# A softmax load of which one row is sent over 126 and 2 partitions, so that DMA engines 14 and 15 carry less

## Chip, cores and metric

One core of one Trainium2 chip. Times are device microseconds of one launch. Executions are sorted into a fast and a slow state by their time and clock. A comparison runs a kernel and the kernel before in turn on the same chip; its ratio has a 95% interval. The kernel before had 162.26 us (162.17 to 162.34, 3 runs) when the prediction was made.

## The reference

```python
def reference(x):                     # x: 16 x 1024 x 512, float32
    x_scaled = x / 2.0
    x_max = np.max(x_scaled, axis=-1, keepdims=True)
    exp_x = np.exp(x_scaled - x_max)
    return (exp_x / np.sum(exp_x, axis=-1, keepdims=True)).astype(np.float32)
```

33.55 MB are read and as many written.

## The kernel before

The 16384 rows are cut into 12 tiles of 3, 7, 15 ... 15, 7, 3 and 3 rows per partition. A tile is loaded by one DMA over 128 partitions, worked on in place and stored by one DMA. Eight loads are issued from the scalar engine at the start; stores and the last four loads come from the sync engine, so there are two queues. The vector engine takes the maximum (`do_max`), the scalar engine the exponential and its sum, the vector engine multiplies by the reciprocal.

```python
PLAN = [
    ([3], 0), ([4, 3], 3), ([5] * 3, 10), ([5] * 3, 25), ([5] * 3, 40), ([5] * 3, 55),
    ([5] * 3, 70), ([5] * 3, 85), ([5] * 3, 10), ([4, 3], 3), ([3], 0), ([3], 25),
]
# ... cut
    def issue_loads(begin, end):
        for t in range(begin, end):
            if t not in behind:      # behind: tiles whose place another tile must leave first
                nc.scalar.dma_start(out=sb(t), in_=dram(xf, t)).then_inc(ld[t], 16)

    def do_max(k):
        t, b, c, a = chunks[k]
        nc.vector.reduce_max(
            out=negmax[:, b : b + c], in_=arena[:, a : a + c],
            axis=mybir.AxisListType.X, negate=True,
        )._wait_ge(ld[t], 16).then_inc(s_max, 1)
# ... cut: reciprocal, multiply, exponentials
        for t in range(len(tiles)):
            nc.sync.wait_ge(s_mul, last_chunk[t] + 1)
            nc.sync.dma_start(out=dram(of, t), in_=sb(t)).then_inc(
                st[t] if t in awaited else s_end, 16
            )
            # ... cut: late loads, each behind the stores that free its place
```

## Time and profile before

| | before |
|---|---|
| time, us | 162.26 |
| span of the profiled execution, us | 161.7 (that execution took 163.47 in all) |
| vector / scalar engine busy, us | 131.7 / 94.5 |
| end of the vector engine's work, us | 143.6 |
| end of the last DMA data packet, us | 160.29 |

How the profile is read stands in the prediction. The profiled execution was 1.2 us longer than the timed ones.

### The profile page before, as it was taken

The numbers are of one execution on the slowest core, as the hardware profiler recorded it, in microseconds if no ns is written. First come the engines' busy times: TensorE is split into PE (matmuls) and PEld (weight loads), VectorE is DVE, ScalarE is ACT, GpSimd is POOL, SyncE is SP. The second block draws the span as 40 slices with busy tenths as digits, with TensorE's granted clock in tenths as the row PEclk, the third lists the DMA queues.
The fourth block names the chain that finished last, engine by engine and source line by source line (L and its number), as shares of the span: only waits on it lengthen the run. The fifth ranks groups of instructions, "written<-read, shape, count | busy, mean of one in ns | idle before, by whom it ended". The sixth has DMA issues, their size and how long they took to land.

```text
span 161.7 us, 480 instructions
## 1 busy us (share of the span) xinstructions
DVE 131.7 (81%) x155; ACT 94.5 (58%) x257; POOL 0.2 (0%) x4
## 2 busy tenths in 40 slices
DVE  0475599999999999999999999999999999950000
ACT  0739086748646745976667866668766875600000
POOL 0000000000000000000000000000000000000000
DMA  7989999899999899999999999999999899999991
GB/s 283 464 388 464 410 436 438 326 466 404 473 380 479 372 486 410 441 448 405 456 395 471 388 471 405 448 399 457 409 412 482 388 471 426 426 448 403 414 414 53
DMA packets 3459, 67.13 MB, mean 415 GB/s; under 512 B 384, under 2 KB 384, under 8 KB 1152
## 3 DMA queue, kind: packets, MB, share of 16 engines
q1 hardware_dynamic: 2304, 40.90, 59.0%
q10 hardware_dynamic: 1152, 26.21, 38.5%
q14 instruction: 3, 0.02, 0.0%
HBM read 33.55 MB, written 33.55 MB: 415 GB/s over the span
## 4 chain that ended last, share of the span: by engine, by line
DVE 77%; DMA 10%; issue 0%; DVEq 0%
DVE negmax L89 40%; DVE arena L109 22%; DVE arena L102 13%; DMA arena<-in_x_dram 10%; DVE recip L98 2%; DVEq L204 0%
## 5 line engine op out<-in xcount | busy, mean ns | idle before, releaser
L122 ACT ACTIVATE arena<-arena,negmax 128x512 f32<-128x512 f32 x128 | 90.7, 710 | 42.6 <-DVE negmax L89 42.6
L89 DVE TENSOR_REDUCE negmax<-arena 128x5 f32<-128x2560 f32 (+2 forms) x28 | 72.3, 2585 | 10.9 <-DMA arena<-in_x_dram 10.9
L109 DVE TENSOR_SCALAR arena<-arena,recip 128x512 f32<-128x512 f32 x91 | 37.8, 482 | 0.7
L122 ACT ACTIVATION_READ_ACCUMULATOR arena<-arena,negmax 128x1 f32 x128 | 23.9, 187 | 0.0
L102 DVE TENSOR_TENSOR arena<-arena,recip 128x2560 f32<-128x2560 f32 (+2 forms) x8 | 21.0, 2625 | 0.3
L98 DVE RECIPROCAL recip<-sums 128x5 f32<-128x5 f32 (+2 forms) x28 | 4.9, 176 | 0.0
L122 ACT ACT_TABLE_LOAD x1 | 1.3, 1283 | 4.6 <-issue 4.6
L193 POOL MEMSET const-bfloat16-1.0<- 128x1 bf16 x1 | 0.1, 102 | 0.0
L193 POOL MEMSET const-uint8-127<- 128x1 uint8 x1 | 0.1, 102 | 0.0
L193 POOL MEMSET const-float32-0.0<- 128x1 f32 x1 | 0.1, 99 | 0.2 <-issue 0.2
L193 POOL MEMSET const-float32-1.0<- 128x1 f32 x1 | 0.1, 99 | 0.0
## 6 DMA issues: line engine op xcount, KB each, us to landing
out_dram<-arena SPq DMA_DIRECT2D x7, 3840.0 KB, 22.9
arena<-in_x_dram ACTq DMA_DIRECT2D x6, 3840.0 KB, 46.9
arena<-in_x_dram SPq DMA_DIRECT2D x1, 3840.0 KB, 30.4
out_dram<-arena SPq DMA_DIRECT2D x2, 1792.0 KB, 16.6
out_dram<-arena SPq DMA_DIRECT2D x3, 768.0 KB, 15.8
arena<-in_x_dram ACTq DMA_DIRECT2D x1, 1792.0 KB, 8.3
arena<-in_x_dram SPq DMA_DIRECT2D x1, 1792.0 KB, 34.0
arena<-in_x_dram SPq DMA_DIRECT2D x2, 768.0 KB, 34.8
```

Of the source, the lines that this page charges most:

```text
L89: nc.vector.reduce_max(out=negmax[:, b : b + c], in_=arena[:, a : a + c], axis=mybir.AxisListType.X, negate=True,)._wait_ge(ld[t], 16).the ...
L98: nc.vector.reciprocal(out=recip[:, b : b + c], in_=sums[:, b : b + c])._wait_ge(s_exp, k + 1).then_inc(s_rec, 1)
L102: nc.vector.tensor_mul(out=arena[:, a : a + c], in0=arena[:, a : a + c], in1=recip[:, b : b + c].unsqueeze(2).to_broadcast([P, c, D]),)._w ...
L109: ins = nc.vector.tensor_scalar_mul(out=arena[:, a + r], in0=arena[:, a + r], scalar1=recip[:, b + r : b + r + 1],)
L122: ins = nc.scalar.activation(out=arena[:, a + r], in_=arena[:, a + r], func=mybir.ActivationFunctionType.Exp, bias=negmax[:, b + r : b + r ...
L193: nc = _bacc.Bacc("TRN2", target_bir_lowering=False, num_devices=1)
```

## The change

The intent is to take work off DMA engines 14 and 15. One row of the second load goes over 126 partitions by a DMA of its own, and the last two partitions of that row by a third DMA; the prediction says why this should spare engines 14 and 15.

```diff
+SPREAD = 1
@@ issue_loads
-            if t not in behind:
+            if t == SPREAD:
+                r = tiles[t][1] - 1
+                for p, q, lo, hi in ((0, P, 0, r), (0, 126, r, r + 1), (126, P, r, r + 1)):
+                    nc.scalar.dma_start(
+                        out=sb(t)[p:q, lo:hi], in_=dram(xf, t)[p:q, lo:hi]
+                    ).then_inc(ld[t], 16)
+            elif t not in behind:
                 nc.scalar.dma_start(out=sb(t), in_=dram(xf, t)).then_inc(ld[t], 16)
@@ do_max
-        )._wait_ge(ld[t], 16).then_inc(s_max, 1)
+        )._wait_ge(ld[t], 48 if t == SPREAD else 16).then_inc(s_max, 1)
```

## The prediction

> **What bounds the kernel now.** I read the first two parts of the page first: the busy shares and the forty slices of about 4.04 us each.
>
> ```profile
> span 161.7 us, 480 instructions
> DVE 131.7 (81%) x155; ACT 94.5 (58%) x257; POOL 0.2 (0%) x4
> DVE  0475599999999999999999999999999999950000
> ACT  0739086748646745976667866668766875600000
> DMA  7989999899999899999999999999999899999991
> HBM read 33.55 MB, written 33.55 MB: 415 GB/s over the span
> ```
>
> The reader is to see that the vector engine falls silent four slices (some 17 us) before the end, while the DMA row stays at 9 until the last slice. Transfers end this kernel, not arithmetic. The chain of waits on the page says "DVE 77%" and hides this: its last piece is a vector multiply that ends near 143.6 us, because the final wait for all stores is not followed back to a transfer. So I left the chain and looked at the window sums (columns: stretch, its length, busy time of the three engines, clock, DMA share, GB/s).
>
> ```profile
> 1.00:1.50 0.50, 0.00 (x0) 0.00 (x0) 0.00 (x0) 1.00 1.00 172
> 1.50:2.00 0.50, 0.00 (x0) 0.00 (x0) 0.00 (x0) 1.00 0.56 184
> ...
> 157.00:157.60 0.60, 0.00 (x0) 0.00 (x0) 0.00 (x0) 1.00 1.03 430
> 157.60:158.20 0.60, 0.00 (x0) 0.00 (x0) 0.00 (x0) 1.00 0.50 205
> 158.20:158.80 0.60, 0.00 (x0) 0.00 (x0) 0.00 (x0) 1.00 0.27 113
> 158.80:159.40 0.60, 0.00 (x0) 0.00 (x0) 0.00 (x0) 1.00 0.12 51
> 159.40:160.30 0.90, 0.00 (x0) 0.00 (x0) 0.00 (x0) 1.00 0.05 20
> ```
>
> The tail is the point. Up to 157.6 us all 16 DMA engines work; then the share falls to 0.50, 0.27, 0.12 and 0.05, and 0.05 of 16 engines is less than one engine. The end of the kernel is set by one DMA engine that is late, over two microseconds after most of the others. The change shifts bytes between engines, so only this imbalance can pay.
>
> **Which engine is late.** The trace also holds every packet (start, duration, size) and every semaphore increment of a DMA, but not the engine's number. I joined packets into 16 series, each packet following the end of another by at most a few ns. The first packets of the first load start at 1.14 to 1.47 us on fourteen engines and at 2.00 and 2.02 us on two. The increments of the second load arrive at a median of 8.21 us; the last three are 0.37, 0.62 and 0.68 us behind it. So two engines are some 0.65 us late there, and keep it: the third load has two at 0.86 and 0.88, the fourth two at 1.07. In the last phase, when one queue alone is left, the last increments lie 0.57, 0.81, 0.87 and 1.48 us behind the median at 106 us, and 0.62, 0.86, 1.34 and 2.22 us at the very end (median 158.4 us). The step from 1.48 to about 2.2 and from 0.87 to about 1.35 comes near 111 to 112 us, where a few 6144-byte load packets take 402 to 915 ns in place of 234. The 16 series end at 160.29, 159.40, 158.94, 158.69, and the rest from 157.6 to 158.2 us.
>
> **What the Trainium skill says.** In "DMA: Bandwidth & Descriptors", section "Why a DMA increments its semaphore by 16 and not by 1", a DMA issued from the scalar or sync engine runs on the largest k up to 16 that divides the slowest dimension of both sides, on the lowest-numbered k engines. So 126 partitions go to 14 engines, nine each; 2 partitions go to engines 0 and 1; and engines 14 and 15 get nothing of that row. Before, every transfer has 128 partitions and 16 increments of its own, which agrees, but no transfer of the kernel before has another k. The same section says that the sequencer writes the missing 16 − k increments itself, so that waiting for 48 over the three parts is complete. The section "Latency and other measured facts" calls engines 7 and 15 usually slower, and ties it to descriptors written by GpSimd; this kernel has none of those, and the trace shows two late engines but cannot name them. The section "Issuing engines are not separate DMA queues" says that sequencers share the same 16 engines, so extra issues gain no bandwidth; 1.00 to 1.01 of DMA share through the middle of the run agrees.
>
> **The change part by part.**
>
> Packet cost. Undisturbed packets take 1138 ns for 30720 bytes, 535 ns for 14336 and 234 ns for 6144. A row of 2048 bytes is worth (1138 − 535) / 8 = 75.4 ns on its engine, with 535 − 7 × 75.4 = 7 ns per packet on top. A lone row should thus cost about 83 ns (an estimate from these three), a six-row packet about 460 ns.
>
> Engines 14 and 15: eight packets of seven rows become eight of six rows. They lose 8 × 75.4 = 603 ns each, which is close to the 0.62 to 0.68 us by which two engines are late at the second load. This match is why I believe the intent is to level two late starters.
>
> Engines 0 to 13: they lose the same 603 ns and gain nine lone rows, 9 × 83 = 747 ns, and one 4-byte increment packet of 9 ns: about +0.15 us. Engines 0 and 1 gain one row and one increment more: about +0.24 us. In sum the change adds 12 × 0.15 + 2 × 0.24 − 2 × 0.60 = 1.1 us of engine time, 0.07 us averaged over 16: nothing is saved but the imbalance.
>
> Issue cost. Eight loads are issued on the scalar queue between 0.13 and 4.54 us, at about 0.33 to 0.74 us each (median 0.47).
>
> ```profile
> L85 ACTq DMA_DIRECT2D arena<-in_x_dram x8: 335/466/737, 0.1 to 4.1; - x8
> 4.57 1.28 ACT L122 ACT_TABLE_LOAD   x1 [4.57 <-issue]
> 6.41 0.72 ACT L122 ACTIVATE arena<-arena,negmax 128x512 f32<-128x512 f32 x1 [0.56 <-DVE negmax L89]
> 8.91 3.95 DVE L89 TENSOR_REDUCE negmax<-arena 128x4 f32<-128x2048 f32 x2 [2.53 <-DMA arena<-in_x_dram]
> ```
>
> The lines are of the view of one source line and of the timeline at the start. Two more issues put the table load off by some 0.9 us, from 4.57 to about 5.5, its end from 5.85 to about 6.8, and the first exponential from 6.41 to about 6.8. The second load lands on the slowest of the fuller engines, so the maximum at 8.91 starts 0.1 to 0.3 us later, and the first store (issued at 14.28) follows by as much. None of it is on the path to the end: the vector engine ends its work 17 us before the transfers do, and from 2 us on the engines always have loads queued.
>
> The path to the end. If the last series (160.29) is engine 14 or 15, it ends 0.60 us sooner, at 159.69. The next, if it is the other of the two, ends at 158.80; if not, at 159.40 + 0.15 = 159.55; either way the last still sets the end, and the gain is 0.60 us. If the last series is another engine, the end moves back by 0.15 us. I give the first 0.75, the second 0.25: 0.75 × (−0.60) + 0.25 × 0.15 = −0.41 us, which from 162.26 us is about 161.85 us.
>
> **The rivals.** First, the late end comes from elsewhere: half of the last engine's lateness came after 106 us with slow packets, which may fall to any engine on another schedule. For it speaks the step of 0.7 to 0.8 us near 111 us; against it, that two series were late without a break from the first load to the end. It would give 162.3 to 162.5 us. Second, the lateness feeds itself: engines already late meet the slow packets because they are late. Then levelling them at the start takes the later steps away too, down to where the third series (158.94 + 0.15) sets the end: 1.2 us less, about 161.1 us. For it speaks that the largest steps fell on the two latest; against it, that these are few events. I put a little weight here, and it moves my number to 161.8 us. Third, the start becomes the bound: short packets or extra issues leave engines without work before the third load is queued. It needs a hole in the first 8 us; the window 4 to 8 us has a DMA share above 1, with 3.6 us of queued seven-row packets to cover one microsecond of issue. Were it real, it would cost up to 0.5 us, 162.8 us.
>
> **The range and the chances.** The three runs before span 0.17 us, so the spread is in the mechanism, not in noise. The cases run from 161.1 to 162.8 us, with most of the weight from 161.5 to 162.4; I take 161.2 to 162.5. A change of 2% is 3.2 us. The whole tail after 158 us is 2.3 us, so even perfect balance can't reach 2%, and nothing added comes near it either: faster 0.01, within 2% 0.98, slower 0.01.
>
> **What would show each step right or wrong.** Right: 126 packets of 2048 bytes on 14 series and two on two others, near 83 ns each; two series that lack them; the second load's increments without two stragglers at 0.6 us; the last DMA packet near 159.7 us in place of 160.29; table load near 5.5 us. Wrong: the late series carry the extra rows (the wrong engines relieved, time up by 0.15 us or more); the early stragglers gone, yet one late at the end as before (the lateness was made later); or 2048-byte packets much slower than 83 ns.

## The result

The changed kernel took 162.64 us (162.53 to 162.94, 4 runs), the kernel before in the same rounds 162.30 us (162.17 to 162.68, 4 runs): ratio 1.002, interval 0.9998 to 1.0042. A ratio here is the mean time of one kernel's fast runs over that of the other's of the same rounds, so not quite the ratio of the medians. The time lies outside the predicted range of 161.2 to 162.5, on the slow side, though "within 2%" holds.

The profile after, first the busy rows of the page:

```profile
span 161.2 us, 482 instructions
DVE  0466499999999999999999999999999999960000
DMA  7998999999999998989899999989989999999892
```

Nothing has changed in kind: the vector engine is silent at the end, DMA is not. Then the window sums of the changed kernel (stretch, length, busy time of DVE, ACT and POOL, clock, DMA share, GB/s):

```profile
157.00:157.60 0.60, 0.00 (x0) 0.00 (x0) 0.00 (x0) 1.00 0.95 399
157.60:158.20 0.60, 0.00 (x0) 0.00 (x0) 0.00 (x0) 1.00 0.60 246
158.20:158.80 0.60, 0.00 (x0) 0.00 (x0) 0.00 (x0) 1.00 0.12 51
158.80:159.40 0.60, 0.00 (x0) 0.00 (x0) 0.00 (x0) 1.00 0.07 31
159.40:160.30 0.90, 0.00 (x0) 0.00 (x0) 0.00 (x0) 1.00 0.02 7
```

The share at 158.20 has fallen from 0.27 to 0.12: fewer engines are late. But 0.07 of 16 engines is still one engine, up to 159.4 us. The tail is thinner, not gone. And its end, 159.76 us for the last data packet, is earlier than the 160.29 us of the profile before, while the timed runs are slower. Two profiles thus say the opposite of eight timed runs, so one profile of each kernel was not enough.

The start, in the timeline of the changed kernel:

```profile
0.55 1.43 ACTq L90 DMA_DIRECT2D arena<-in_x_dram  x3
5.38 1.28 ACT L131 ACT_TABLE_LOAD   x1 [5.38 <-issue]
9.33 3.94 DVE L98 TENSOR_REDUCE negmax<-arena 128x4 f32<-128x2048 f32 x2 [3.08 <-DMA arena<-in_x_dram]
```

The table load moved by 0.8 us as predicted (0.9), the second maximum by 0.42 us (predicted 0.1 to 0.3).

One more view, of both kernels, over the stretch in which the second and third loads land. Before:

```profile
6.00:12.00 6.00, 3.47 (x3) 2.99 (x9) 0.00 (x0) 1.00 1.05 450
12.00:20.00 8.00, 4.20 (x6) 4.27 (x13) 0.00 (x0) 1.00 1.04 433
20.00:28.00 8.00, 7.93 (x7) 5.62 (x15) 0.00 (x0) 1.00 0.93 398
28.00:36.00 8.00, 7.96 (x4) 5.29 (x16) 0.00 (x0) 1.00 1.07 438
```

After:

```profile
6.00:12.00 6.00, 2.92 (x3) 3.24 (x8) 0.00 (x0) 1.00 1.09 432
12.00:20.00 8.00, 4.41 (x6) 4.69 (x14) 0.00 (x0) 1.00 0.94 405
20.00:28.00 8.00, 7.93 (x7) 5.41 (x15) 0.00 (x0) 1.00 1.00 430
28.00:36.00 8.00, 7.97 (x5) 5.50 (x16) 0.00 (x0) 1.00 1.08 455
```

The last column is to be read downwards. The change loses 18 and 28 GB/s in the first two stretches, and wins 32 and 17 GB/s in the next two. In bytes: before 6 x 450 + 8 x (433 + 398 + 438) = 12852 kB, after 6 x 432 + 8 x (405 + 430 + 455) = 12912 kB. A real cost at the start, 0.6 us at the third load, is given back by 36 us as far as these windows show. (When an engine has done its share of a DMA it adds one to the DMA's semaphore; a transfer over 128 partitions has 16 such increments in the trace.) In all five profiles of the change the median increment of the third load comes at 17.98 to 18.08 us, against 17.31 to 17.42 us in the four of before; the median of the very last store is nearly the same (158.28 to 158.40 us in the three profiles of before without tags in the middle, 158.30 to 158.49 us in four of the change).

### The profile page after: what moved, and what is told of

It reads as the page before. It is cut to its first block, busy times and chain, and to the rows that moved or that the text cites. A ratio compares the mean times of both kernels' runs of the same rounds, so it can differ in the third digit from the quotient of the medians.

```text
span 161.2 us, 482 instructions
## 1 busy us (share of the span) xinstructions
DVE 131.7 (82%) x155; ACT 94.5 (59%) x257; POOL 0.2 (0%) x4
## 4 chain that ended last, share of the span: by engine, by line
DVE 77%; DMA 10%; issue 0%; DVEq 0%
DVE negmax L98 40%; DVE arena L118 22%; DVE arena L111 13%; DMA arena<-in_x_dram 10%; DVE recip L107 2%; DVEq L213 0%
```

## The experiments

The theories, by the letters that the expectations use:

- A: in an ordinary execution an engine other than 14 and 15 ends last, and only the added packets on 0 to 13 count. (In the first call it also stood for "the late end was chance".)
- B: the late starters 14 and 15 end last, and the relief works. This is the prediction.
- C: splitting the load costs, by issues and short packets.
- D, E: a transfer over 126 partitions is slow wherever it stands (D), or only at the start (E). G: short packets are slow in any layout.
- F: before, 14 or 15 ends last; after, 0 or 1 does.
- H, I: the tenth row on engines 0 and 1 makes one of them end last (H), or that engine's own lateness and nine rows suffice (I).

Eighteen runs were made, on four chips. All passed the comparison with the reference.

### 1. Both kernels again

No edit.

> The kernel before, unchanged, as a null test and for a second profile. The profile of before that I predicted from was taken in an execution of 163.47 us, 1.2 us over its timed median of 162.26. Theory A (the late end in that profile was a chance event of that execution): the ratio is 1.000 within 0.001, and the new profile shows no packet of 900 ns near 111 us, or another one elsewhere, and the last packet 0.8 to 1.2 us after the median of the last increments, not 2.2. Theory B (the late end is the rule, always on the same two late-starting engines): the last increment again lies about 2.2 us behind the median.

> The changed kernel, unchanged, with more rounds. Theory A (in an ordinary execution an engine out of 0 to 13 ends last, so that only the +0.15 to +0.24 us of their added packets count): ratio 1.001 to 1.0015 against before. Theory C (the split itself costs, by two more issues and short packets at the start): ratio 1.002 to 1.003. Theory B (the relief works): 0.996 to 0.998.

Measured: before again 162.32 us against 162.72 us for the same kernel in the same rounds, ratio 0.9974 (0.9949 to 0.9999). The change 163.13 us, ratio 1.0019 (0.9995 to 1.0044). Two things follow. A kernel against itself gave 0.26%, and its interval misses 1, so one comparison of five rounds decides nothing below 0.3%, and the intervals are somewhat too narrow. For the change, B (0.996 to 0.998) is out; A and C both lie within the interval. And the second profile of before ends its last data packet at 159.61 us, not 160.29: the profile that the prediction was read from was a long one. Of its late packets the one of 915 ns near 111 us is gone (306 ns over usual is the worst there after 105 us). The last increment lies 1.67 us behind the median, between what the two theories said. The changed kernel ended at 160.08 us in its second profile, later than in its first.

### 2. The same three transfers, evenly over all engines

```diff
-for p, q, lo, hi in ((0, P, 0, r), (0, 126, r, r + 1), (126, P, r, r + 1)):
+for p, q, lo, hi in ((0, P, 0, r), (0, 64, r, r + 1), (64, P, r, r + 1)):
```

> Control: the same three transfers for the second load, but the lone row over partitions 0 to 63 and 64 to 127, so that all 16 engines carry eight rows of it and no engine is relieved. Issues, short packets and the wait for 48 are as in the change. Theory A: the added cost is 16 packets' overhead at 7 ns less, some 0.06 to 0.08 us, ratio 1.0004. Theory C: as slow as the change, 1.002 to 1.003. Two engines should still be 0.6 us late at the second and third load.

Measured: 162.77 us, ratio 0.9997 (0.9973 to 1.0022), in the same rounds in which the change had 163.13 us. The slow start is there too: third load at 18.09 us, and by the windows 420 GB/s from 6 to 12 us and 422 from 12 to 20. So neither the issues nor the slow start show in the time, though a cost of 0.2% would still fit the interval. The 0.36 us between this kernel and the change, and its last data packet at 159.52 us (159.76 to 160.08 in the change), point at the uneven rows, but the two intervals overlap.

### 3. Four rows in place of one

```diff
-r = tiles[t][1] - 1
-((0, P, 0, r), (0, 126, r, r + 1), (126, P, r, r + 1))
+r = tiles[t][1] - 4
+((0, P, 0, r), (0, 126, r, r + 4), (126, P, r, r + 4))
```

> Dose: four rows instead of one go over 126 and 2 partitions. Engines 14 and 15 lose 32 rows, 2.4 us; engines 2 to 13 gain 9 x (4 x 75.4 + 7) - 8 x 4 x 75.4 = 0.37 us, engines 0 and 1 0.68 us (estimates from the packet times). Theory A: +0.37 to +0.68 us, ratio 1.0023 to 1.0042. Theory C (cost of the split, not of the dose): as the change itself, 1.002. Theory B: the last engines are relieved, so 0.998 to 1.002. The series of engines 14 and 15 should end 2 us ahead of the rest and so be told by name.

Measured: 164.29 us, ratio 1.0097 (1.0073 to 1.0120): some 1.6 us, over twice what theory A's bytes give. Engines 14 and 15 show up by their lead: two increments of the third load come 1.8 us ahead of the median. The window from 6 to 12 us of this kernel:

```profile
6.00:12.00 6.00, 0.76 (x2) 2.94 (x7) 0.00 (x0) 1.00 1.08 300
```

A DMA share above 1 at 300 GB/s: the engines count as busy and move a third less. The 8192-byte packets took 473 ns in the mean, where (from 30720 and 14336 bytes) 309 ns were to be expected, and the first packets of the third load took 1.6 to 2.7 us, not 1.14. At this dose the loss is no longer given back: the median of the last store comes at 160.07 us, 1.7 us late.

### 4. Whole transfers of the same sizes

Both parts over 128 partitions; first with four rows in the second part, then with one.

```diff
-((0, P, 0, r), (0, 126, r, r + 1), (126, P, r, r + 1))
+((0, P, 0, r), (0, P, r, r + 4))      # r = rows - 4; wait for 32
```

> Control for the dose of four: the second load in two transfers of all 128 partitions, rows 0 to 2 and rows 3 to 6, every engine with the same bytes as before. Theory D (the transfer over 126 partitions itself is slow, at some 240 GB/s in its stretch, because its packets are not laid out as those of 128 partitions are): ratio 1.000 within 0.002, and 8192-byte packets at 310 ns. Theory C (splitting a load at the start costs): 1.003 or more, with slow 8192-byte packets as in the run of four rows over 126 partitions, where they took 473 ns in the mean.

Measured: 162.79 us, ratio 1.0021 (0.9992 to 1.0051). 8192-byte packets 315 ns in the mean, third load at 17.43 us, as before the change. The window to set beside that of run 3:

```profile
6.00:12.00 6.00, 3.38 (x3) 3.25 (x10) 0.00 (x0) 1.00 1.06 454
```

```diff
+((0, P, 0, r), (0, P, r, r + 1))      # r = rows - 1; wait for 32
```

> Control for the short packets: the second load as six rows and one row, both over all 128 partitions and 16 engines, so that 128 packets of 2048 bytes run as in the change, but each engine keeps its own partitions. In the three profiles of the change the first packet of the third load took 1.39 to 1.68 us on all engines in place of 1.14, and the third load landed at 18.0 to 18.1 us in place of 17.3 to 17.4. Theory D (the cost comes from the layout over 126 partitions): first packets at 1.14 to 1.3 us, third load at 17.4. Theory G (it comes from short packets in any layout): 1.4 to 1.6 us, third load near 18. Time in both cases within 0.3% of before.

Measured: 162.79 us, ratio 1.0010 (0.9979 to 1.0041). 128 packets of 2048 bytes; the first packets of the third load 1138 ns at the median, third load at 17.48 us. In the five profiles of the change those first packets were 1.50 to 1.62 us. So theory G falls, and C for the start: short packets over 128 partitions slow nothing that is seen there; the same packets over 126 partitions (or over two halves, run 2) slow the stretch by about 0.6 us. Theory D holds for the load at the start. Why the layout does it no run shows. In time these two controls are not told apart from the change: their last data packets ended at 159.67 and 159.77 us, about where the earliest of the change did.

### 5. Four rows, on the eighth load

```diff
-SPREAD = 1
+SPREAD = 7      # and four rows, as in run 3
```

> The dose of four on the eighth load in place of the second, far from the start, its bytes otherwise the same. Theory D (the cost is that of the 126-partition transfer and falls on engines 0 to 13, wherever it stands): +1.0 to +1.7 us, ratio 1.006 to 1.010. Theory E (the cost is one of the start, where nothing else is in flight): only the estimated bytes, +0.37 to +0.68 us, ratio 1.002 to 1.004.

Measured: 166.61 us, ratio 1.0257 (1.0228 to 1.0287), 4 us and more, beyond both theories. The waits of this kernel, and the place in its timeline:

```profile
DVE negmax L98 <- DMA arena<-in_x_dram: 21.8, 4, 11.0
...
107.39 2.82 DVE L98 TENSOR_REDUCE negmax<-arena 128x5 f32<-128x2560 f32 x1 [11.02 <-DMA arena<-in_x_dram]
```

The vector engine, which is never short of data here in the kernel before, stands for 11.0 us before this tile. The median increment of its load came at 91.3 us before; the last part of it landed at 107.4 us now. The cut load shares the engines with 30720-byte packets of the stores. The Trainium skill, "DMA: Bandwidth & Descriptors", section "Queues, rings and completion order", says that an engine takes turns between its queues by packets; then the queue with the smaller packets gets less, and with 8192-byte packets against 30720-byte ones the load falls behind. The trace agrees: on the engines that could be followed, load and store packets alternate almost one by one from 74 to 102 us. The cut load has 17 packets on an engine in place of 8; nine more turns of at least 1.14 us are 10 us (an estimate), and the median of its last 16 increments came 12.6 us later, at 103.9 us. For D against E the time is spoilt by this wait. But the windows speak against E; first before, then this run:

```profile
93.00:110.00 17.00, 16.86 (x26) 11.82 (x34) 0.00 (x0) 1.00 0.99 427
93.00:110.00 17.00, 5.95 (x8) 3.64 (x10) 0.00 (x0) 1.00 0.99 373
```

The engines were as busy and moved less, and most store packets that began near 96, 98, 100 and 101.6 us took 1.4 to 1.7 us in place of 1.14: slow packets are not confined to the start.

### 6. Naming the engines

The trace does not number DMA engines. Tags do: tiny loads of k partitions, each k with its own size, queued behind the last store. By the rule that the prediction took from the Trainium skill (the largest k that divides, on the lowest-numbered engines), a DMA of k partitions (k up to 16) runs on engines 0 to k - 1, and the trace has k tag packets of each k; so the first tag after an engine's last data packet tells its number; engines 0 and 1 stay one name. The second pair has tags at 97 and 132 us too.

```diff
+for k in range(2, 17):
+    nc.sync.dma_start(out=tags[0:k, 36 * k : 37 * k + 20], in_=xf[0:k, 0 : 20 + k]).then_inc(s_tag, 16)
+nc.gpsimd.wait_ge(s_tag, 240)
```

> A label on the engines: the kernel before, with fifteen tiny loads of k partitions (k = 2 to 16, each k with its own packet size of 4 x (20 + k) bytes) queued behind the last store, so that engine e carries the tags of all k above e and the packet series can be named. Time a little longer, correct. Theory B (the late starters end last): the last data packet of the last store is on engine 14 or 15. Theory A (another engine ends last): it is on one of 0 to 13, while 14 and 15 stand 0.5 to 0.9 us behind the median at most.

> The same tags behind the changed kernel. Theory A: the last engine is one of 0 to 13 and 1.3 to 2 us behind the median, as in the two profiles of the change so far; 14 and 15 are level with the median or ahead of it. Theory B: 14 or 15 last.

> The kernel before with tags at three places: behind the fifth store (some 97 us, one queue alone left), behind the seventh store (some 132 us) and behind the last. The first tagged profile of before had engine 15 last, 1.27 us behind the median, engine 14 0.86, engine 3 and one of engines 0 and 1 0.6. Theory F (on before the late starters 14 and 15 end last, and the latest of them is delayed once more by the 6144-byte loads between 106 and 124 us): engine 15 or 14 again last, 1.2 to 2.2 us behind; 14 and 15 late at the first tags too, and the last one's lateness grows by 0.3 to 0.8 us between the first and second tags. Theory A (any engine may end last): another one.

> The same tags on the changed kernel. The first tagged profile of it had engine 0 or 1 last, at 1.7 us behind the median, and 14 and 15 in the pack. Theory F: engine 0 or 1 again, 1.0 to 1.3 us behind at the first tags already, and later by 0.3 to 0.8 us at the second. Theory A: another engine.

The times (164.42 and 164.91 us for before, 165.82 and 165.69 us for the change) hold the tags and are not compared. What each engine's last data packet ended at, in us, worked out from the tags:

| | 15 | 14 | 0 or 1, the later | 3 | median of the increments |
|---|---|---|---|---|---|
| before | **159.36** | 158.95 | 158.70 | 158.71 | 158.39 |
| before, second | 158.74 | 159.10 | **159.17** | 158.99 | 158.64 |
| change | by 158.9 | by 158.4 | **160.08** | 158.81 | 158.44 |
| change, second | by 158.8 | 158.1 | **159.99** | 158.73 | 158.57 |

("By": some engines paused between data and tags, so only a bound can be given.) Before, engines 14 and 15 do belong to the tail, but engine 0 or 1 is close behind or even ahead. After, 14 and 15 are in the pack, as intended, and engine 0 or 1 ends 0.8 to 1.4 us later than before. F names the last engine rightly in three profiles of four; it fails in the second of before, and A (an engine other than 14 and 15) in the first. F also expected engine 0 or 1 of the change 1.0 to 1.3 us behind at 97 us, which did not come.

Where does that engine lose it? The place of its tag at 97 us was 0.16 us behind the median in the second profile of before and 0.33 us in that of the change; at 132 us 0.9 and 1.8 us. So most of it comes between 97 and 132 us, long after the changed load.

Part of it can be named. The page of every profile has a third queue, which by its name brings instructions and which the readings so far passed over:

```profile
q14 instruction: 3, 0.02, 0.0%
```

Its three packets of 8192 bytes come near 30 to 33, 75 to 78 and 98 to 100 us in every kept trace. At 97 us, just before the third, the tags name engines 0 and 1 in four profiles (the second pair, and the two tagged ones of run 7). In all four the third packet starts within 4 ns of the end of a packet on the later of engines 0 and 1. It takes 309 to 559 ns, and the store packet behind it 1349 to 1451 ns in place of 1138: 0.63 us lost in the second profile of before, 0.64 us in that of the change. In before this is nearly all of the 0.7 us by which the engine fell back between the two tags; in the change it fell back 1.5 us, of which another 0.42 us is one 6144-byte load packet of 652 ns at 123.1 us. The instruction queue thus helps to put engine 0 or 1 into the tail of both kernels. Why it falls back further in the changed one it does not say.

### 7. Without the tenth row on engines 0 and 1

First by two transfers of one partition each, then (the first failed in its aim) by leaving the row out.

```diff
-... (126, P, r, r + 1))
+... (126, 127, r, r + 1), (127, P, r, r + 1))      # wait for 64
```

> The change with the last two partitions of the lone row loaded by two transfers of one partition each, whose 512 elements should run on 16 engines in pieces of 128 bytes, in place of one transfer on engines 0 and 1. Theory H (the row that engines 0 and 1 get on top is what makes one of them end last): the last increment comes at 159.4 to 159.9 us as in before, ratio 0.998 to 1.001. Theory I (that engine is late for other reasons, and the nine rows and the slow stretch after them suffice): last at 160.0 to 160.5 us, ratio 1.001 to 1.003.

> The same with tags at 97, 132 us and at the end. Theory H: engine 0 or 1 at most 0.9 us behind the median at the end, as in the tagged profiles of before (0.6 and 0.9). Theory I: 1.4 to 1.7 us behind, as in the tagged profiles of the change.

Measured: 162.95 us, ratio 1.0027 (1.0008 to 1.0045). The trace shows 128 packets of 2048 bytes, none of 128 bytes: each of the two transfers ran whole on one engine, so engine 0 had eleven lone rows, not nine. The last data packet ended at 159.84 us; with tags engine 0 or 1 ended last at 159.53 us. Nothing is told apart by this.

```diff
-... (126, P, r, r + 1))
+nc.gpsimd.memset(sb(t)[:, r : r + 1], 0.0).then_inc(s_zero, 1)   # the scalar queue waits for it
+... (0, 126, r, r + 1))                                           # and no third transfer
```

> Wrong on purpose in two partitions of one row: the change without its transfer over the last two partitions (that row is set to zero on GpSimd first, so its outputs in partitions 126 and 127 are wrong). Engines 0 and 1 then carry nine lone rows like 2 to 13, not ten. The attempt to spare them with one-partition transfers failed: each of those ran on one engine only. Theory H (the tenth row makes engine 0 or 1 end last): last data packet at 159.2 to 159.6 us, ratio 0.998 to 1.001. Theory I (the nine rows and that engine's own lateness suffice): last data packet 159.7 to 160.1 us as in the change (159.76 to 160.08), ratio 1.001 to 1.003.

> The same with tags. Theory H: engine 0 or 1 at most 0.9 us behind the median at the end. Theory I: engine 0 or 1 last again, 1.2 to 1.7 us behind. Wrong in the same two partitions on purpose.

Measured: 162.72 us, ratio 1.0023 (0.9998 to 1.0047), the last data packet at 159.80 us; with tags at 159.82 us, on engine 0 or 1 again, 1.5 us behind the median engine, with engine 3 next at 159.64 us. (256 KB of the row less 4 KB are loaded; the wrong values in two partitions of one row lay within the comparison's tolerance.) Theory H fails in both profiles: engine 0 or 1 ends last without the tenth row. That agrees with I, though one comparison can't tell the ratios of H and I apart. Of that engine's 1.35 us between the tags at 97 and 132 us, the instruction packet and the packet behind it took 0.62 us, two slow 6144-byte packets (415 and 719 ns) 0.67 us; why it meets slow ones remains unexplained.

### 8. The change once more, and a candidate

> The changed kernel once more, to narrow the interval. The two comparisons so far gave 1.0020 and 1.0019 with intervals that just include 1. Pooled with this one I expect 1.002, that is +0.3 to +0.4 us, and the last increment of its profile at 160.0 to 160.5 us.

Measured: 163.09 us against 162.46 us, ratio 1.0030 (1.0008 to 1.0051), last data packet at 159.89 us. The three comparisons of the change, weighted by the inverse square of their intervals, give 1.0023, with an interval of about 1.0010 to 1.0036. The run of before against itself was off by as much (0.26%), so a small loss is likely rather than shown.

The candidate gives the relief where engines 14 and 15 end, in the last store, behind which there is no other work.

```diff
+if t == len(tiles) - 1:
+    r = tiles[t][1] - 1
+    for p, q, lo, hi in ((0, P, 0, r), (0, 126, r, r + 1), (126, P, r, r + 1)):
+        nc.sync.dma_start(out=dram(of, t)[p:q, lo:hi], in_=sb(t)[p:q, lo:hi]).then_inc(s_end, 16)
```

> A candidate: the kernel before, but one row of the last store, not of a load, goes over 126 and 2 partitions. Engines 14 and 15 lose 8 x 75 = 0.6 us at the place where they end last, nothing waits for the transfer but the end. By the tagged profile of before: engine 15 from 159.36 to 158.8, engine 0 or 1 from 158.70 to 158.95 (estimates), so the end 0.4 us sooner, ratio 0.9975. If the transfer over 126 partitions is slow on the store side too, as on the load side (0.3 to 0.5 us), it is 1.000 to 1.002.

> The candidate once more, unchanged: one row of the last store over 126 and 2 partitions. It gave 0.9983 (0.9961 to 1.0004), with the last increment at 159.3 us. If the gain is real, again 0.997 to 0.999, and pooled an interval below 1; if it was a chance of that session, 1.000.

Measured: 162.32 us against 162.67 us, ratio 0.9983 (0.9961 to 1.0004), and 162.19 us against 162.46 us, ratio 0.9984 (0.9965 to 1.0003). Weighted as above: 0.9984, about 0.9970 to 0.9998. The tail of the first of the two:

```profile
157.00:157.60 0.60, 0.00 (x0) 0.00 (x0) 0.00 (x0) 1.00 0.99 396
157.60:158.20 0.60, 0.00 (x0) 0.00 (x0) 0.00 (x0) 1.00 0.78 304
158.20:158.80 0.60, 0.00 (x0) 0.00 (x0) 0.00 (x0) 1.00 0.22 85
158.80:159.40 0.60, 0.00 (x0) 0.00 (x0) 0.00 (x0) 1.00 0.01 3
```

Here the share is 0.78 where the change had 0.60, and 0.01 where it had 0.07: the same end work, on more engines, over sooner. The last data packet ended at 158.91 and 158.86 us. All 128 packets of 2048 bytes took 84 ns and all of 4096 bytes 159 ns: the store over 126 partitions was not slowed as the load was. This version is a quarter of a microsecond ahead of before by two comparisons, which is at the edge of what these runs can tell; of the changed forms only this one and run 2 (0.9997) did not come out slower.

## Why the prediction was wrong

**The bound** was right. No compute wait of the start came through to the end, and the end was set by one late DMA engine in every profile of the change.

**The step that failed** is in "the path to the end": "If the last series (160.29) is engine 14 or 15, it ends 0.60 us sooner", with the next engine at 159.40 + 0.15. This took the distances of one profile for the rule. That execution was 1.2 us over the timed runs. In the next three profiles of before the last packet ended at 159.61, 159.36 and 159.17 us. By the tags, 0.66 us lay between engine 15 and the latest engine outside 14 and 15 in one of them, and in the other such an engine was last already. By the prediction's own costs there was some 0.4 us to win in the first (159.36 less 158.70 + 0.24), and nothing in the other. And engine 0 or 1, whose end was to move by 0.24 us, ended at 160.0 to 160.1 us.

**The other term that failed** is the cost on the engines that take the rows. They were given +0.15 us, engines 0 and 1 +0.24 us. Measured, the later of engines 0 and 1 went from 158.70 and 159.17 us to 160.08 and 159.99 us. The mean end of the last data packet went from 159.61 us (four profiles of before: 160.29, 159.61, 159.36, 159.17) to 159.96 us (five of the change: 159.76, 160.08, 159.89, 160.08, 159.99), +0.35 us, which is the size of the timed loss; the four of before spread over 1.1 us, so these means alone prove little. The first rival, "the late end comes from elsewhere", foresaw 162.3 to 162.5 us; with 162.64 and 1.0023 even that was a little short. The range was missed by 0.14 us, less than the 0.4 us between two runs of the same kernel in run 1: it is the tags that show the step wrong, not this distance.

**The packet costs** were right as records and wrong as a sum. The 2048-byte packets took 84 ns at the median (83 estimated), on 14 engines and two. But the slowing shows in the packet behind them, at the median 1.50 to 1.62 us in place of 1.14, on all engines. No sum of packet records of the kernel before could show it; a transfer over 126 partitions was not in that trace. At one row no effect on the end is seen (run 2 has it and 0.9997); at four rows the time was 1.6 us longer, against 0.37 to 0.68 us by the sum of packets.

**The levelling** was right: with the change the increments of the third load lie within 0.2 to 0.35 us above the median, where before two were 0.6 us late. In run 2, where no engine is relieved, the two stay late (0.58 and 0.86 us). So the late starters are engines 14 and 15, as claimed; they were simply not the only ones that mattered.

**The rival "lateness feeds itself"** gained some support, without proof: in all five profiles of the change the latest engine falls back by a further 0.5 to 0.8 us between the increments at 106 and at 123 us, in those of before by 0 to 0.7 us. Whether being late is the cause is open, as is why engine 0 or 1 falls back more in the changed kernel.

**Slips of reading.** Two loads are named one too early: two increments lie 0.55 and 0.60 us behind at the third load, 0.86 and 0.88 us at the fourth, 1.07 us at the fifth. The lateness that came after 106 us is 0.74 of 2.22 us, a third and not half. And eight queued packets of seven rows are 4.3 us, of six rows 3.7 us, not 3.6. None of them moves the number.

## What to carry to other kernels

When the end hangs on one of 16 DMA engines, relieving the engine that was last in one trace may only hand the end to the next one, as here; take several profiles and name the engines (with tags of known size) before shifting bytes, see how far behind the next one is, and look for small queues that load a single engine. Relief seems better placed at the end of the stream, where no later work can undo it: the same row moved in the last store gave -0.16%, in the second load +0.23%, both near the limit of these runs. And cut a load along its rows, not along its partitions: four rows cut off cost 0.2% over 128 partitions (an interval with 1 in it) and 1.0% over 126 and 2.

## What the Trainium skill lacked or had wrong

- "DMA: Bandwidth & Descriptors", section "Why a DMA increments its semaphore by 16 and not by 1": right for 126 and 2 partitions. The second load's semaphore had one increment at 1.8 us and one at 2.1 us, before any data, as the section says of the 16 - k, then 14 and 2 more. For a transfer of one partition of 512 elements I took from it that 16 engines share it; the trace shows one packet of 2048 bytes on one engine.
- Same page, "Latency and other measured facts": it calls engines 7 and 15 usually slower and ties that, as a guess, to descriptors written by GpSimd. There are none here, yet two engines start at 2.0 us where the others start at 1.1 to 1.5, and the levelling by the change says that these are 14 and 15; engine 7 was the first to finish (157.7 us) in the tagged profile of before. Engine 15 does end last in one profile of two.
- Neither this page nor "SBUF — State Buffer" has a figure for what a load over 126 partitions does to the transfers beside it. Measured: 300 GB/s from 6 to 12 us with four rows over 126 partitions, against 454 with the same rows over 128, and, with one row, first packets of the next load at 1.50 to 1.62 us, not 1.14.
- No page tells how far the engines of one transfer drift apart: after nearly 160 us of equal tensor bytes their ends lay 1.6 and 1.1 us apart in the two tagged profiles of before.
- No page says which engine the packets of the instruction queue fall on, or what they cost: 309 to 559 ns on engine 0 or 1 near 98 us, and 0.2 to 0.3 us more on the packet behind.
